# Decay matrices from differences of cumulative decays, with rows spread by DMA

## The chip, the cores and the metric

The kernel runs on one core of a Trainium2 chip. A core has TensorE (PE in the profile; its weight loads are PEld), VectorE (DVE), ScalarE (ACT), GpSimd (POOL) and SyncE (SP, which here only issues DMAs). Each engine works through its own queue in order and waits on semaphores for the others. The metric is the device time of one execution in microseconds; the median of 3 runs of the kernel before is 1635.08 us (1632.72 to 1635.48).

## What is computed

The reference is one layer of a diffusion backbone over 1024 latent tokens and 256 context tokens of width 1024. One input projection feeds two groups of heads: a bidirectional gated DeltaNet (4 heads of 128) and a two-dimensional neighbourhood attention (8 heads of 64); then come an output projection and a SwiGLU block. The change is in the DeltaNet, whose chunked form is, for each head and direction:

```
gam = cumsum(g)                                  # g = log of the decay, within a chunk
decay = exp(where(tril, gam[i] - gam[j], -inf))  # a triangle of decays
m = where(strict, (beta * k) @ k.T * decay, 0)
u, w = solve(I + m, beta * v), solve(I + m, beta * k * exp(gam))
qk = where(tril, q @ k.T * decay, 0)
S, o = scan over the chunks with u, w, qk, gam, and the last gam of a chunk
```

Both directions are scanned; the backward one takes the triangle the other way round. Context chunks come first in each direction. The kernel uses chunks of 128 tokens where the reference has 64, which gives the same sums.

## The kernel before, in words

The kernel is written in a framework that schedules: the Python code says what is computed, and a scheduler sets the order of the instructions on each engine by priorities and estimates of its own. Nearly all DMAs are issued by SyncE, in one queue. A DMA that has to wait (for a free buffer, or for data) holds all DMAs behind it in that queue. Tiles come from pools with a number of buffers for each name; an allocation beyond that number waits until the oldest tile of the name has been used for the last time, its store to memory included.

There are 10 chunks of 128 tokens (2 of context, 8 latent), 4 heads and 2 directions. The tables of one token and head (`G` the log decays, `NB` minus the normalised beta, `EG`, `KD`, `ET` exponentials of sums) are made once by `decay_tables` (L712) for all chunks, with few and small instructions one after the other; `block_inverses` (L765) inverts the 32x32 diagonal blocks of I + m and leaves them in `x_d`. Then `preps` (L854) makes 20 chunk preparations, one for each chunk and direction. A preparation is for all 4 heads at once and consists of:

- `fetch` (L870): loads of the products `kk` (k with k, 4 buffers) and, for a latent chunk, `at` (q with k, 3 buffers), 256 KB each, and of the diagonal blocks `xc` (3 buffers).
- the decay matrix. GpSimd multiplies `G` with a triangular mask into `rg` (L887), once for the high and once for the low part of `G`, 128x512 each. TensorE sums over them with three matmuls of N = 512 into one PSUM bank: two with the mask `mr` (L897), and one with the identity and `mneg` (L898), which adds −1e30 outside the triangle. ScalarE takes the exponential of the bank into the tile `y` (L901, 4 buffers).
- VectorE multiplies `kk` with it for each head (L903) and `at` for all (L906); the decayed `at` is stored to `at_d` (L930).
- the solve: TensorE (L911), a copy by ScalarE (L913), and three rounds of matmuls (L920) and an addition on VectorE (L921) into the same `y`, which is stored to `y_d` (L930). A later part of the kernel reads `y_d` and `at_d`.

At most three preparations are live and one more is fetched. They are generators, advanced between the pieces of the input projection as background work (`bg.step`, 1 to 5 steps at a time). The projection consists of Blocks (matmuls at L389, weights split into a high and a low part, the low part `wlo` by GpSimd at L199) and Wide blocks (L572, `zlo` at L565; their output goes by `nv_d` stores at L583, and copies within memory spread it into `vw_d` at L1024). Context chunks may be prepared early; a latent chunk is fetched only once the blocks of q are done. In the run before, context preparations lie at about 300 to 345 us, latent ones at 425 to 608 us.

Of the kernel before, what the change touches and what calls it, by code (L numbers as in the profile page):

```python
# [26 lines left out]
NCH = T // 128  # L27
NU = NCH * NH
# [5 lines left out]
C_ID, C_LE, C_GE, C_BD2, C_ONE = range(5)  # L34
# [53 lines left out]
def hybrid(ctx, tc, a, dbg):  # L88
# [26 lines left out]
    def const(name, shape, dt=F32):  # L115
        return mid.tile(shape, dt, name=name, tag=name)
# [7 lines left out]
    ident = M[C_ID]  # L124
# [10 lines left out]
    for i, v in enumerate((EPS, -0.5 * math.log(64.0))):  # L135
        dve.memset(bias[:, i:i + 1], v)
    b_eps, b_naq = bias[:, 0:1], bias[:, 1:2]
    mr = const("mr", [128, 5, 128], F32R)
    mneg = const("mneg", [128, 2, 128], F32R)

    v_d = dram.tile([T, 512], F32, name="v_d", tag="v_d")
    k_d = dram.tile([T, 512], F32, name="k_d", tag="k_d")
# [10 lines left out]
    y_d = dram.tile([2, NCH, 128, 4, 128], F32, name="y_d", tag="y_d")  # L153
    at_d = dram.tile([2, 8, 128, 4, 128], F32, name="at_d", tag="at_d")
    x_d = dram.tile([128, 2, 2, NU, 32], F32, name="x_d", tag="x_d")
    x2_d = dram.tile([KT, 128, L], F32, name="x2_d", tag="x2_d")
    f_d = dram.tile([NFB, 2, 128, 512], F32, name="f_d", tag="f_d")
    t_d = dram.tile([NFB, 2, 128, 512], F32, name="t_d", tag="t_d")
# [14 lines left out]
    EG = const("EG", [128, 2, NCH, 4])  # L173
    KD = const("KD", [128, 2, NCH, 4])
    ET = const("ET", [128, 2, NCH, 4])
    act.activation(sc2, c2, AF.Silu)
    bg = Background()

# [181 lines left out]
    with ExitStack() as bs:  # L360
# [242 lines left out]
        with ExitStack() as xs:  # L603
# [26 lines left out]
            wide = xp.tile([128, KT, 32], F32, name="wide", tag="wide")  # L630
            pool.memset(wide, 0.0)
            pool.tensor_copy(wide[:, :, 0:2], sc2)
            pool.tensor_copy(mr[:, 4], ident)
            for d in range(2):
                pool.tensor_scalar(mneg[:, d], masks[:, d], -1.0e30, None, op0=OP.mult)
            pool.tensor_copy(mr[:, 0:4], masks)
            rs = xp.tile([128, T], F32, name="rs", tag="rs")
            acc = xp.tile([128, T], F32, name="acc", tag="acc")
# [73 lines left out]
        def decay_tables(gp):  # L712
            def small(name):
                return gp.tile([128, 2, NCH, 4], F32, name=name, tag=name)
            A, S, E, P2, X = (small(n) for n in ("gA", "gS", "gE", "gP", "gX"))
            nA = gp.tile([128, 8], F32, name="nA", tag="nA")
            act.activation(nA, adt[:, 0:8], AF.Exp)
            dve.tensor_scalar(nA, nA, -1.0, None, op0=OP.mult)
            for d in range(2):
                dtb = adt[:, 8 + 4 * d:12 + 4 * d].rearrange("p (o h) -> p o h", o=1).to_broadcast([128, NCH, 4])  # L720
                dve.tensor_tensor(A[:, d], ab[:, :, 4 * d:4 * d + 4], dtb, OP.add)
            dve.tensor_scalar(X, A, -1.0, None, op0=OP.mult)
            dve.tensor_tensor(X, X, A, OP.max)
# [12 lines left out]
            dve.scalar_tensor_tensor(A, P2, 2.0, A, op0=OP.mult, op1=OP.add)  # L736
            for d in range(2):
                nb = nA[:, 4 * d:4 * d + 4].rearrange("p (o h) -> p o h", o=1).to_broadcast([128, NCH, 4])
                dve.tensor_tensor(G[:, d], A[:, d], nb, OP.mult)
            dve.tensor_scalar(B, B, 1.0, None, op0=OP.add)  # L740
            dve.reciprocal(B, B)

            Y = gp.tile([128, 2, NCH, 4], F32, name="gY", tag="gY")
            dve.tensor_scalar(SV, SV, EPS, None, op0=OP.add)
            rsqrt(Y[:, 0], SV, Y[:, 1])
            dve.tensor_tensor(SV, SV, Y[:, 0], OP.mult)
            dve.tensor_tensor(Y[:, 0], Y[:, 0], Y[:, 0], OP.mult)
            for d in range(2):
                dve.tensor_tensor(B[:, d], B[:, d], Y[:, 0], OP.mult)
            dve.tensor_scalar(NB, B, -1.0, None, op0=OP.mult)  # L750
            dve.tensor_copy(GH, G)
            dve.tensor_tensor(GL, G, GH.bitcast(F32), OP.subtract)
            for _ in range(4):
                yield
            pg = bank()
            for d in range(2):
                g = G[:, d].rearrange("p c h -> p (c h)")
                for q, m in enumerate((M[C_LE + d], mr[:, d].bitcast(F32), M[C_ONE])):
                    o = (q * 2 + d) * NU
# [94 lines left out]
        def preps():  # L854

            first_half.close()
            with ExitStack() as gs:
# [4 lines left out]
                def work(name, bufs=2, dt=F32):  # L862
                    return (pk if name == "kk" else pp).tile([128, 4, 128], dt, name=name, tag=name, bufs=bufs)
# [5 lines left out]
                def fetch(d, c):  # L869

                    kk, xc = work("kk", 4), pp.tile([128, 2, 4, 32], F32, name="xc", tag="xc", bufs=3)
                    sp.dma_start(kk, kk_d[:, c])
                    sp.dma_start(xc, x_d[:, d, :, c * 4:c * 4 + 4])
                    at = None
                    if c >= 2:
                        at = work("at", 3)
                        sp.dma_start(at, qk_d[:, c - 2])
                    return d, c, kk, xc, at

                def prep(n, d, c, kk, xc, at):  # L880
                    lat = c >= 2
                    mle = M[C_LE + d].rearrange("p (o i) -> p o i", o=1).to_broadcast([128, 4, 128])
                    rgs = []
                    for gg in (GH, GL):
                        rg = work("rg", 2, F32R)
                        src = gg.bitcast(F32)[:, d, c].rearrange("p (h o) -> p h o", o=1).to_broadcast([128, 4, 128])
                        pool.tensor_tensor(rg, src, mle, OP.mult)  # L887
                        rgs.append(rg)
                    x0, fx = x0s[n % 3], fxs[n % 2]
                    for b in range(4):  # L890
                        q = slice(b * 32, b * 32 + 32)
                        act.copy(fx[q, :, q], xc[q, 1])
                        pool.tensor_copy(x0[q, :, q], xc[q, 0])
                    yield 1
                    p = bank("pr")
                    for j, rg in enumerate(rgs):
                        pe.matmul(p, mr[:, d], fl(rg), start=j == 0, stop=False)  # L897
                    pe.matmul(p, mr[:, 4], mneg[:, d].rearrange("p (o i) -> p o i", o=1).to_broadcast([128, 4, 128]),  # L898
                              start=False, stop=True)
                    e = work("y", 4)  # L900
                    act.activation(fl(e), p, AF.Exp)  # L901
                    for h in range(4):
                        dve.scalar_tensor_tensor(kk[:, h], kk[:, h], NB[:, d, c, h:h + 1], e[:, h],  # L903
                                                 op0=OP.mult, op1=OP.mult)
                    if lat:
                        dve.tensor_tensor(at, at, e, OP.mult)  # L906
                        stores.append((at_d[d, c - 2], at, tick[0] + 2))
                    yield 1
                    p = bank("pr")
                    for h in range(4):  # L910
                        pe.matmul(p[:, hs[h]], kk[:, h], fx[:, h], start=True, stop=True)  # L911
                    f = kk
                    act.copy(fl(f), p)  # L913
                    yield 1
                    y = e
                    src = x0
                    for _ in range(3):
                        p = bank("pr")
                        for h in range(4):
                            pe.matmul(p[:, hs[h]], f[:, h], src[:, h], start=True, stop=True)  # L920
                        dve.tensor_tensor(fl(y), p, fl(x0), OP.add)  # L921
# [725 lines left out]
```

## Time and profile before

| | us |
|---|---|
| median of 3 runs | 1635.08 (1632.72 to 1635.48) |
| span of the profiled execution | 1634.2 |
| TensorE busy | 1525.4 (93%) |
| VectorE busy | 1037.2 (63%) |
| ScalarE busy | 705.7 (43%) |
| GpSimd busy | 203.0 (12%) |

The profile gives no other time for its execution than the span from the first to the last instruction; the median of the runs is 0.9 us longer. A group's line names the line of the code, the engine, the operation, the tile written and the tiles read, the shape, the number of instructions, then busy time in us and the mean of one in ns, then the idle time of that engine just ahead of them and what ended it. A window's line gives its start and end, its length, and for each engine the busy time and the number of instructions, then the granted TensorE clock as a share of full speed, the share of the DMA engines in use and what they moved in GB/s. In the timeline the columns are the start, the length, the engine, the line, the operation; `[5.59 <-issue]` means 5.59 us of idle time ahead of it, ended by what the arrow names ("issue": by nothing that the profile shows).

### The profile page before, as it was taken

The numbers are of one execution on the slowest core, as the hardware profiler recorded it, in microseconds if no ns is written. First come the engines' busy times: TensorE is split into PE (matmuls) and PEld (weight loads), VectorE is DVE, ScalarE is ACT, GpSimd is POOL, SyncE is SP. The second block draws the span as 40 slices with busy tenths as digits, with TensorE's granted clock in tenths as the row PEclk, the third lists the DMA queues.
The fourth block names the chain that finished last, engine by engine and source line by source line (L and its number), as shares of the span: only waits on it lengthen the run. The fifth ranks groups of instructions, "written<-read, shape, count | busy, mean of one in ns | idle before, by whom it ended". The sixth has DMA issues, their size and how long they took to land.

```text
span 1634.2 us, 24148 instructions
## 1 busy us (share of the span) xinstructions
PE 1525.4 (93%) x8642; PEld 1284.3 (79%) x8642; DVE 1037.2 (63%) x1934; ACT 705.7 (43%) x1340; POOL 203.0 (12%) x275
## 2 busy tenths in 40 slices
PE   3999999999988798999998999999999999999999
PEld 1689787779888786878776787888888888888887
DVE  5855678444364466567898538966565666679752
ACT  5342363663332234565665228433333333445441
POOL 2053611522333220000010000000000000000000
PEclk9998999999999899999998999999999999999999
DMA  9366121535345527999954920532322333798752
GB/s 371 122 195 190 56 75 41 185 120 187 110 131 169 197 93 198 311 276 288 269 175 144 301 102 33 168 123 97 104 97 97 100 107 108 227 364 293 269 162 84
DMA packets 211720, 275.23 MB, mean 168 GB/s; under 512 B 16144, under 2 KB 120080, under 8 KB 210576
## 3 DMA queue, kind: packets, MB, share of 16 engines
q1 hardware_dynamic: 210736, 273.06, 51.6%
q8 instruction: 68, 1.11, 0.3%
q10 hardware_dynamic: 864, 0.63, 0.1%
q14 instruction: 52, 0.43, 0.1%
HBM read 206.78 MB, written 71.04 MB: 170 GB/s over the span
## 4 chain that ended last, share of the span: by engine, by line
PE 64%; DMA 5%; DVE 5%; ACT 3%; issue 2%; SPq 1%; POOL 0%; DVEq 0%; ACTq 0%
PE ps L1219 25%; PE ps L1566 13%; PE blk L389 4%; PE ps L1350 3%; PE blk L572 3%; PE pr L920 2%; PE sc L317 2%; DMA at_d<-at 2%; PE sc L307 2%; PE sc L295 2%; PE ps L1112 1%; DVE cacc L445 1%; PE ps L1372 1%; PE ps L1124 1%; PE pr L911 1%
## 5 line engine op out<-in xcount | busy, mean ns | idle before, releaser
L389 PE MATMUL blk<-hh,whi 128*128 128x512 f32 (+1 forms) x416 | 126.6, 398 | 3.4 <-ACT whi L198 1.6
L389 PE MATMUL blk<-hh,wlo 128*128 128x512 f32 (+1 forms) x416 | 120.4, 383 | 2.3 <-POOL wlo L199 2.3
L1280 ACT CAST uhi<-ws 128x512 fp32r<-128x512 f32 x91 | 54.8, 623 | 151.4 <-PE ps L1219 72.8
L1280 ACT CAST uhi<-wq 128x512 fp32r<-128x512 f32 x101 | 60.6, 621 | 134.9 <-issue 61.6
L389 PE MATMUL blk<-hl,whi 128*128 128x512 f32 (+1 forms) x416 | 117.3, 380 | 0.0
L1281 DVE TENSOR_TENSOR ulo<-wq,uhi 128x512 fp32r<-128x512 f32 x101 | 67.5, 688 | 66.3 <-ACT uhi L1280 36.1
L1219 PE MATMUL ps<-hT,uhi 128*128 128x512 f32 x336 | 104.1, 391 | 3.1 <-ACT hT L1398 3.1
L1219 PE MATMUL ps<-lT,uhi 128*128 128x512 f32 x336 | 104.0, 391 | 0.0
L1219 PE MATMUL ps<-hT,ulo 128*128 128x512 f32 x336 | 103.5, 389 | 0.0
L572 PE MATMUL blk<-zhi,hh 128*128 128x256 f32 (+2 forms) x304 | 90.8, 299 | 0.0
L389 PEld LDWEIGHTS blk<-hh,wlo 128*128 128x128 f32 x416 | 75.2, 196 | 19.2 <-POOL wlo L199 2.8
L1219 PE MATMUL ps<-hB,uhi 128*128 128x512 f32 x288 | 89.7, 392 | 0.0
L1219 PE MATMUL ps<-lB,uhi 128*128 128x512 f32 x288 | 89.3, 391 | 0.0
L1219 PE MATMUL ps<-hB,ulo 128*128 128x512 f32 x288 | 88.8, 389 | 0.0
L572 PE MATMUL blk<-zhi,hl 128*128 128x256 f32 (+2 forms) x304 | 88.4, 291 | 0.0
L572 PE MATMUL blk<-zlo,hh 128*128 128x256 f32 (+2 forms) x304 | 87.9, 289 | 0.0
L389 PEld LDWEIGHTS blk<-hh,whi 128*128 128x128 f32 x416 | 72.7, 198 | 18.4 <-issue 3.6
L389 PEld LDWEIGHTS blk<-hl,whi 128*128 128x128 f32 x416 | 75.0, 196 | 14.1 <-DVE hl L690 0.3
L1281 DVE TENSOR_TENSOR ulo<-ws,uhi 128x512 fp32r<-128x512 f32 x91 | 60.8, 687 | 37.6 <-ACT uhi L1280 29.3
L903 DVE SCALAR_TENSOR_TENSOR kk<-kk,NB,y 128x128 f32<-128x128 f32 x80 | 37.8, 529 | 62.5 <-ACT y L901 62.5
L198 ACT CAST whi<-wraw 128x1024 fp32r<-128x1024 f32 x26 | 27.3, 1049 | 116.0 <-PE blk L389 48.8
L1219 PEld LDWEIGHTS ps<-hT,uhi 128*128 128x128 f32 x336 | 63.0, 188 | 16.3 <-ACT hT L1398 3.5
(333 smaller groups left out, 3778.3 us busy)
## 6 DMA issues: line engine op xcount, KB each, us to landing
wq<-w_fo SPq DMA_DIRECT2D x99, 256.0 KB
wq<-w_gu SPq DMA_DIRECT2D x88, 256.0 KB
wad<-wa SPq DMA_DIRECT2D x64, 256.0 KB
bt<-rpb SPq DMA_DIRECT2D x64, 192.0 KB
t_d<-g SPq DMA_DIRECT2D x22, 512.0 KB
fr<-t_d SPq DMA_DIRECT2D x44, 256.0 KB
f_d<-g SPq DMA_DIRECT2D x33, 256.0 KB
fr<-f_d SPq DMA_DIRECT2D x33, 256.0 KB
```

Of the source, the lines that this page charges most:

```text
L295: pe.matmul(sc[:, u * 640 + n0:u * 640 + n1], q, ks[i], start=i == 0, stop=i == 1)
L307: pe.transpose(sc[:, u * 640 + j * 128:u * 640 + (j + 1) * 128], bt[:, j * 128:(j + 1) * 128], ident)
L317: pe.matmul(sc[u * ND:u * ND + ND, 1280:1408], vv, pt[:, j * 128:(j + 1) * 128], start=j == 0, stop=j == 4)
L389: pe.matmul(o, ww[:, k], xx[k][:, s], start=k == 0 and j == 0, stop=k == KT - 1 and j == end)
L572: pe.matmul(p[:, :c1 - c0], x[k][:, s], ww[:, k, c0:c1], start=k == 0 and j == 0, stop=k == KT - 1 and j == 2)
L903: dve.scalar_tensor_tensor(kk[:, h], kk[:, h], NB[:, d, c, h:h + 1], e[:, h], op0=OP.mult, op1=OP.mult)
L920: pe.matmul(p[:, hs[h]], f[:, h], src[:, h], start=True, stop=True)
L1219: pe.matmul(o, w[wi][:, k], x[xi][:, k], start=first and k == 0 and j == 0, stop=k == n - 1 and j == 2, skip_group_check=True)
L1280: act.copy(hi, self.raw[key])
L1281: dve.tensor_tensor(lo, self.raw[key], hi.bitcast(F32), OP.subtract)
L1350: pe.matmul(o, w[wi][:, k], parts[xi][k][:, s], start=k == 0 and j == 0, stop=k == KT - 1 and j == 2)
L1566: pe.matmul(o[b], w[wi][:, b], F[xn, p][xi], start=n in (0, 1, 5) and p == 0 and j == 0, stop=p == NFB // 2 - 1 and j == 2, skip_group_che ...
```

## The change

The decay matrix is taken from differences of cumulative sums. `decay_tables` clamps `G` from below at −110 and keeps the negated sum `GN` for each token; it also transposes the sums, so that each chunk and head is a row of 128, and stores these 80 rows in memory (`g_d`). `fetch` loads the four rows of a chunk, 2 KB, into all 128 partitions of `e` (a `y` tile, now allocated at the fetch, with 5 buffers), 256 KB in SBUF. GpSimd's affine_select fills −1e30 outside the triangle, in place. ScalarE takes the exponential for each head, 128x128, with the column of `GN` as a bias. The three matmuls, `rg` and `mneg` are gone, and `mr` loses its fifth slice; the rest of the preparation is as it was.

```diff
-    mr = const("mr", [128, 5, 128], F32R)
-    mneg = const("mneg", [128, 2, 128], F32R)
+    mr = const("mr", [128, 4, 128], F32R)
...
+    g_d = dram.tile([2 * NU, 128], F32, name="g_d", tag="g_d")
...
+    GN = const("GN", [128, 2, NCH, 4])
...
-            pool.tensor_copy(mr[:, 4], ident)
-            for d in range(2):
-                pool.tensor_scalar(mneg[:, d], masks[:, d], -1.0e30, None, op0=OP.mult)
...
+            dve.tensor_scalar(G, G, -110.0, None, op0=OP.max)
...
+            gn = GN.rearrange("p d c h -> p (d c h)")
+            act.activation(gn, pg[:, :2 * NU], AF.Copy, scale=-1.0)
+            yield
+            p, rows = bank(), gp.tile([128, 128], F32, name="rows", tag="rows")
+            pe.transpose(p[:2 * NU, :128], gn, ident)
+            act.activation(rows[:2 * NU], p[:2 * NU, :128], AF.Copy, scale=-1.0)
+            sp.dma_start(g_d, rows[:2 * NU])
             yield
...
                     sp.dma_start(xc, x_d[:, d, :, c * 4:c * 4 + 4])
+                    e = work("y", 5)
+                    u = (d * NCH + c) * 4
+                    sp.dma_start(fl(e), g_d[u:u + 4].rearrange("h t -> (h t)").partition_broadcast(128))
                     at = None
...
-                    mle = M[C_LE + d].rearrange("p (o i) -> p o i", o=1).to_broadcast([128, 4, 128])
-                    rgs = []
-                    for gg in (GH, GL):
-                        rg = work("rg", 2, F32R)
-                        src = gg.bitcast(F32)[:, d, c].rearrange("p (h o) -> p h o", o=1).to_broadcast([128, 4, 128])
-                        pool.tensor_tensor(rg, src, mle, OP.mult)
-                        rgs.append(rg)
+
+                    pool.affine_select(e, e, pattern=[[0, 4], [1 - 2 * d, 128]], compare_op=OP.is_ge, fill=-1.0e30,
+                                       base=0, channel_multiplier=2 * d - 1)
...
-                    p = bank("pr")
-                    for j, rg in enumerate(rgs):
-                        pe.matmul(p, mr[:, d], fl(rg), start=j == 0, stop=False)
-                    pe.matmul(p, mr[:, 4], mneg[:, d].rearrange("p (o i) -> p o i", o=1).to_broadcast([128, 4, 128]),
-                              start=False, stop=True)
-                    e = work("y", 4)
-                    act.activation(fl(e), p, AF.Exp)
+                    for h in range(4):
+                        act.activation(e[:, h], e[:, h], AF.Exp, bias=GN[:, d, c, h:h + 1])
```

The change also moves instructions. On TensorE the preparations' first matmuls leave the blocks. In a Block of the projection before, with `blk` its banks, `hh` the high part of the activations and `pr` the preparation's bank, there stood:

```order
L389 MATMUL blk_3486<-hh0_133,wlo_3147 128x512
L897 MATMUL pr_3521<-rg_3502,mr_83 128x512
L897 MATMUL pr_3521<-rg_3504,mr_83 128x512
L898 MATMUL pr_3521<-mneg_84,mr_83 128x512
L389 MATMUL blk_3484<-hh1_135,whi_3146 128x256
```

In the changed kernel no such matmul stands there; the preparation's next ones (L911) come in the same Block:

```order
L390 MATMUL blk_3485<-hh1_136,wlo_3148 128x256
L390 MATMUL blk_3486<-hh1_136,wlo_3148 128x512
L390 MATMUL blk_3487<-hh1_136,wlo_3148 128x512
L911 MATMUL pr_3563<-fx0_2314,kk_3497 128x128 x4
L390 MATMUL blk_3485<-hh2_138,whi_3147 128x256
L390 MATMUL blk_3486<-hh2_138,whi_3147 128x512
```

The L911 matmuls of the first latent chunk now stand where the three matmuls of its decay matrix stood.

On VectorE, after the normalisation of q (`RQ2`), the first latent chunks stood like this before (`y` is the decay matrix, at L921 the solve's tile):

```order
L903 SCALAR_TENSOR_TENSOR kk_3496<-kk_3496,NB_115,y_3525 128x128 x4
L906 TENSOR_TENSOR at_3500<-at_3500,y_3525 128x512
L903 SCALAR_TENSOR_TENSOR kk_3514<-kk_3514,NB_115,y_3570 128x128 x4
L906 TENSOR_TENSOR at_3518<-at_3518,y_3570 128x512
L921 TENSOR_TENSOR y_3525<-pr_3605,x01_2298 128x512
L903 SCALAR_TENSOR_TENSOR kk_3553<-kk_3553,NB_115,y_3621 128x128 x4
L906 TENSOR_TENSOR at_3557<-at_3557,y_3621 128x512
L921 TENSOR_TENSOR y_3525<-pr_3637,x01_2298 128x512
```

In the changed kernel the same place reads:

```order
L1033 TENSOR_TENSOR RQ2_110<-RQ_109 128x32
L906 TENSOR_TENSOR at_3503<-at_3503,y_3501 128x512
L906 TENSOR_TENSOR at_3522<-at_3522,y_3520 128x512
L906 TENSOR_TENSOR at_3560<-at_3560,y_3558 128x512
L906 TENSOR_TENSOR at_3604<-at_3604,y_3602 128x512
L906 TENSOR_TENSOR at_3747<-at_3747,y_3745 128x512
L921 TENSOR_TENSOR y_3501<-pr_3607,x01_2312 128x512
```

The products L903 of the first four of them have moved some 40 rows up, ahead of the last convolutions (L442, L446) and just behind the context chunks.

On SyncE, in the second half of the latent chunks, the queue read before:

```order
L877 DMA at_4398<-qk_d_91 128x512
L583 DMA nv_d_92<-zt_4244 128x256
L872 DMA kk_4335<-kk_d_90 128x512
L930 DMA y_d_97<-y_4051 128x512
L873 DMA xc_4459<-x_d_99 128x2x128
L872 DMA kk_4394<-kk_d_90 128x512
L930 DMA y_d_97<-y_4116 128x512
```

In the changed kernel, in the copies' part, with the row loads (L882) between:

```order
L1024 DMA vw_d_94<-nv_d_91 128x1x512 x4
L930 DMA at_d_97<-at_4455 128x512
L878 DMA kk_4608<-kk_d_89 128x512
L930 DMA y_d_96<-y_4133 128x512
L879 DMA xc_4691<-x_d_98 128x2x128
L886 DMA at_4696<-qk_d_90 128x512
L930 DMA at_d_97<-at_4614 128x512
L882 DMA y_4650<-g_d_99 128x512
L878 DMA kk_4646<-kk_d_89 128x512
L930 DMA y_d_96<-y_4332 128x512
```

The loads of rows stand behind stores of `y` that they need a buffer from (the row load into y_4650 takes the buffer of y_4133, whose store stands five rows ahead), the `vw_d` copies come four in a row, and the loads and stores of `at` stand two to three chunks further ahead of those copies.

More of the change, by code (lines that the diff above doesn't have):

```diff
@@ L877, in fetch, with prep @@
                         sp.dma_start(at, qk_d[:, c - 2])
-                    return d, c, kk, xc, at
-                def prep(n, d, c, kk, xc, at):
+                    return d, c, kk, xc, e, at
+                def prep(n, d, c, kk, xc, e, at):
                     lat = c >= 2
-                    mle = M[C_LE + d].rearrange("p (o i) -> p o i", o=1).to_broadcast([128, 4, 128])
-                    rgs = []
-                    for gg in (GH, GL):
-                        rg = work("rg", 2, F32R)
-                        src = gg.bitcast(F32)[:, d, c].rearrange("p (h o) -> p h o", o=1).to_broadcast([128, 4, 128])
-                        pool.tensor_tensor(rg, src, mle, OP.mult)
-                        rgs.append(rg)
+                    pool.affine_select(e, e, pattern=[[0, 4], [1 - 2 * d, 128]], compare_op=OP.is_ge, fill=-1.0e30,
+                                       base=0, channel_multiplier=2 * d - 1)
                     x0, fx = x0s[n % 3], fxs[n % 2]
```

## The prediction

> **What bounds the kernel now.** I read the page's first section, then a table of windows over the chunk preparations, then the waits, the chain and single pieces of the timeline there.
>
> ```profile
> span 1634.2 us, 24148 instructions
> PE 1525.4 (93%) x8642; PEld 1284.3 (79%) x8642; DVE 1037.2 (63%) x1934; ACT 705.7 (43%) x1340; POOL 203.0 (12%) x275
> ```
>
> TensorE is busy for 93% of the span, so work taken off TensorE is worth something only where TensorE is what the others wait for. Preparations run in two places, so I cut those into windows.
>
> ```profile
> core 0: us, PE busy (x) PEld busy (x) DVE busy (x) ACT busy (x) POOL busy (x), PEclk, DMA share, GB/s
> 300.00:345.00 45.00, 40.48 (x221) 32.91 (x220) 20.18 (x32) 27.02 (x50) 26.00 (x45) 0.96 0.50 151
> 425.00:450.00 25.00, 22.08 (x123) 18.86 (x122) 11.20 (x15) 10.06 (x19) 13.34 (x9) 0.86 0.43 136
> 450.00:475.00 25.00, 21.49 (x140) 19.78 (x141) 15.46 (x22) 7.07 (x17) 10.53 (x18) 0.93 0.50 154
> 475.00:517.00 42.00, 40.66 (x330) 39.07 (x329) 27.44 (x47) 16.75 (x38) 12.74 (x24) 1.00 0.46 148
> 517.00:575.00 58.00, 44.12 (x281) 39.91 (x281) 19.38 (x39) 12.85 (x33) 16.02 (x30) 0.87 0.54 181
> 575.00:608.00 33.00, 32.17 (x198) 27.45 (x197) 20.62 (x31) 9.06 (x12) 5.84 (x7) 0.97 0.20 70
> ```
>
> Two stretches (475 to 517, 575 to 608) are TensorE's, idle for 1.3 and 0.8 us. From 425 to 475 it idles 50 − 22.08 − 21.49 = 6.4 us, from 517 to 575 58 − 44.12 = 13.9 us. The chain that ended last and SyncE's waits say what those 13.9 us wait for:
>
> ```profile
> 517.08 9.42 DMA at_d<-at
> 540.23 10.88 DMA at_d<-at
> 554.12 10.39 DMA at_d<-at
> 565.43 4.32 DMA y_d<-y
> ```
> ```profile
> SPq L877 <- DMA at_d<-at: 43.3, 10, 8.1
> ```
>
> A store of a decayed product (`at_d`) takes 9 to 11 us here, because it shares the DMA engines with the copies into `vw_d`; the next load into that `at` buffer waits for it on SyncE, and behind it stand the `kk` loads and `y_d` stores. TensorE sees it as two gaps:
>
> ```profile
> 531.50 1.20 PE L911 MATMUL pr<-fx,kk 128*128 128x128 f32 x4 [5.59 <-issue]
> ...
> 570.86 2.08 PE L911 MATMUL pr<-fx,kk 128*128 128x128 f32 x8 [7.38 <-DVE kk L903]
> ```
>
> **The matmuls that go.** Each of 20 preparations loses two matmuls of L897 and one of L898. What they hold of TensorE is the distance from their start to the next matmul's:
>
> ```profile
> 481.96 0.63 PE L897 MATMUL pr<-rg,mr 128*128 128x512 f32 x2
> 482.42 0.39 PE L898 MATMUL pr<-mneg,mr 128*128 128x512 f32 x1
> 482.65 0.28 PE L572 MATMUL blk<-zhi,hh 128*128 128x256 f32 x1
> ```
>
> 482.65 − 481.96 = 0.69 us. The windows of L897 alone (two matmuls a preparation) say where they lie:
>
> ```profile
> 475.00:517.00 42.00, 2.77 (x8) 1.22 (x8) 1.00 0.46 148
> 517.00:575.00 58.00, 4.22 (x10) 1.95 (x10) 0.87 0.54 181
> 575.00:608.00 33.00, 1.78 (x4) 0.96 (x4) 0.97 0.20 70
> ```
>
> Five are in the stretch that is bound by stores; there they fill time that is idle anyway, and I cost them at nothing. The other 15 are worth 15 × 0.69 = 10.4 us. If only the six in the two stretches that are full counted, 4.1 us; if all the busy time of the two lines did, 16.6 + 8.9 = 25.5 us (groups, 300 to 610 us):
>
> ```profile
> L887 POOL TENSOR_TENSOR rg<-GL,cst 128x512 fp32r<-128x512 f32 x20 | 21.2, 1062 | 0.2 <-PE pr L897 0.2
> L887 POOL TENSOR_TENSOR rg<-GH,cst 128x512 fp32r<-128x512 f32 x20 | 21.1, 1055 | 49.5 <-PE pr L897 49.1
> L897 PE MATMUL pr<-rg,mr 128*128 128x512 f32 x40 | 16.6, 486 | 2.1 <-POOL rg L887 2.0
> L898 PE MATMUL pr<-mneg,mr 128*128 128x512 f32 x20 | 8.9, 447 | 0.0
> L901 ACT ACTIVATE y<-pr 128x512 f32<-128x512 f32 x20 | 11.9, 596 | 29.7 <-PE pr L898 20.8 <-DMA y_d<-y 8.7
> ```
>
> I take −10.4, since the busy sum counts the overlap of neighbours twice (0.63 + 0.39 us in the rows above, for 0.69).
>
> **The first latent preparations come earlier.** They no longer need TensorE for the exponent, and on VectorE the first four products with `kk` stand ahead of the last convolutions, 40 rows earlier. What TensorE waits for from 425 to 475 us is such work:
>
> ```profile
> 438.71 1.16 PE L920 MATMUL pr<-x,kk 128*128 128x128 f32 x8 [1.39 <-ACT kk L913]
> ...
> 451.44 1.16 PE L911 MATMUL pr<-fx,kk 128*128 128x128 f32 x8 [1.54 <-DVE y L921]
> ```
>
> Bounds 0 and −6.4; the solve's own sequence (L911, L913, three rounds) stays, and both rows are of it, so −4. What is late next there is L921 on VectorE.
>
> **The stretch bound by stores.** Its ends are −13.9 (all idle time goes) and +30.7 (the three landings of 9.42, 10.88 and 10.39 us come once more). For a gain: the loads and stores of `at` stand two or three chunks further ahead of the `vw_d` copies, so about the two gaps of 5.59 and 7.38 us shrink, less 2 for what the order leaves: −11. Against it: five row loads of 256 KB now fall there, 1.31 MB at the 181 GB/s of the window, 7.2 us. Net −4; nearer to no change than to either end, since the same queue carries the same stores and more.
>
> **The row loads and SyncE.** An issue takes 0.32 us (rows below), so 20 loads take 6.4 us on a queue that does not hold TensorE outside the stretch above. From the sixth latent chunk on, the load needs a `y` buffer that a `y_d` store has to leave, and the store stands two to five places ahead on the same queue. Queued behind the wait are a load of `kk`, stores of `at` and `y` and the Wide blocks' `nv_d` stores. Undisturbed, a store is done in 2.0 us, and `kk` is early by 15 us:
>
> ```profile
> 481.14 0.32 SPq L930 DMA_DIRECT2D at_d<-at  x1
> 483.15 0.32 SPq L877 DMA_DIRECT2D at<-qk_d  x1
> ```
> ```profile
> 454.92 0.32 SPq L872 DMA_DIRECT2D kk<-kk_d  x1
> ```
> ```profile
> 469.93 1.13 DVE L903 SCALAR_TENSOR_TENSOR kk<-kk,NB,y 128x128 f32<-128x128 f32 x4
> ```
>
> So I cost the wait at nothing; the cover is the preparation two or three chunks ahead, and without it each of 11 loads shows up.
>
> **Exponentials.** One of 596 ns becomes four of 128x128 with a pointer as bias; the nearest rows have such an operand:
>
> ```profile
> L1116 ACT ACTIVATE vk<-ps,KN 128x128 f32<-128x128 f32 x64 | 18.7, 371 | 7.5 <-PE ps L1112 7.3
> ```
>
> 20 × (4 × 0.371 − 0.596) = 17.8 us more on ScalarE, which is busy for 40% from 475 to 517 us. ScalarE also evicts TensorE's banks, so a delay of 0.9 us can meet one: +1 (0 to +17.8).
>
> **GpSimd's triangle.** Two products of 1.06 us become one affine_select of 128x512, which the trace does not have. Nearest below is a memset, nearest above a cast of that size:
>
> ```profile
> L867 POOL MEMSET x<- 128x512 f32 x3 | 1.5, 542 | 0.0
> ...
> L636 POOL CAST mr<-masks 128x512 fp32r<-128x512 f32 x1 | 1.7, 1675 | 0.0
> ```
>
> I take 1.1 us, as the product of that size has: GpSimd gains 1 us a chunk and stays off the path, 0. But the select waits for a DMA now, and behind it in program order stand the low parts of weights (`wlo`) that TensorE needs; they have been ahead by whole blocks, so 0.
>
> The Trainium skill (GPSIMD Engine Reference, section 3.1 Elementwise) puts data-dependent branching at about 12 cycles for each element; if the triangle were done so, 512 × 12 / 1.2 GHz is an estimate of 5.1 us for one. No run here shows it, and by it the sum would be that of rival (d).
>
> **VectorE.** Its products run at 347 ns or, beside GpSimd, up to 2460:
>
> ```profile
> L903 DVE SCALAR_TENSOR_TENSOR kk<-kk,NB,y x80: 339/347/2460, 307.8 to 598.6; 128x128 f32<-128x128 f32 x80
> ```
>
> They add up to 37.8 us, 37.8 − 80 × 0.347 = 10 us above the median. With GpSimd's two-input products gone some of that goes: −1 (−10 to 0), as VectorE is mostly off the path.
>
> The Trainium skill (GPSIMD Engine Reference, section 1 Specifications) says that GpSimd shares its SBUF interface with VectorE where that reads two SBUF inputs. The spread of 339 to 2460 ns agrees; by that rule the one-input select would disturb them too, and the sum would be 1 us higher.
>
> **Decay tables.** A clamp, two copies, a transpose and a store of rows come into a serial chain before the preparations, beside TensorE's projection blocks: +0.5 (0 to +3, five steps of some 0.6 us, the exp's 596 ns). The matmul mask's cast and two products at the start leave GpSimd when nobody waits for it: 0.
>
> **Sum.** −10.4 − 4 − 4 + 1 − 1 + 0.5 = −17.9; 1634.2 − 17.9 = 1616.3. The median of the runs, 1635.08 us, is 0.9 above the span, so 1617.
>
> **Rivals.** (a) Both idle stretches vanish, because they were only late preparations: −10.4 − 6.4 − 13.9 + 0.5 = −30.2, 1605. For it: L903 and `issue` end both long gaps. Against: the stores of `at` behind `vw_d` remain.
>
> (b) Gains cancel: ScalarE's delay (up to +17.8) eats them, 1635. Against: ScalarE's share.
>
> (c) SyncE blocks. The row load's wait for the `y_d` store costs 2.0 us in the open and 4.3 (chain, 565 us) to 10.9 in the `vw_d` copies. SyncE already waits through much of this part, so a delay passes to all behind it. It decides when the delays piled up exceed the 15 us that `kk` is early. Eleven loads, six at 2.0 and five at 7.6 (the mean of 4.32 and 10.88) are 50 us; less 15 of cover and the 18 to 23 gained elsewhere, +12: 1647.
>
> (d) The triangle is slow. If one takes three times the cast, 5 us, 20 take 100 us on GpSimd against the 42 of the two products now. Most hides, but in 517 to 575 us, where kk, y and the triangle wait on each other, five show with what they have over the present pair, 5 × (5 − 2.1) = 14.5, and half of the 17.9 is lost because the early start goes: +5.5, 1640. It decides from about 3 us for one. Against: both rows of that size are under 1.7 us.
>
> **How the numbers follow.** Chances: the forecast 0.42 (own range 1608 to 1630), (a) 0.11, (b) 0.08, (c) 0.25, (d) 0.14. A measurement here tells 0.2% (3 us) from no change: the three runs spread by 0.17%. Faster takes the forecast and (a), 0.53; same is (b), 0.08; slower is (c) and (d), 0.39. The range reaches from just below (a), 1604, to just past (c), 1648, and leaves out the upper ends of the unknown costs when several meet.
>
> **What would show it.** Right: no L897 and L898, 475 to 517 shorter by four times 0.69, the gaps at 438 and 451 mostly gone, affine_select near 1.1 us, four exps of about 0.37 us. Wrong: SyncE waiting at L882 for `y_d<-y` for more than 30 us, with TensorE idle at L911 behind it (c); affine_select above 3 us (d); ScalarE's exps releasing TensorE's banks (b); or the waits for `at_d<-at` as long as before, so that the −4 is nothing.

## The result and the profile after

The changed kernel takes 1637.2 us (median of 20 runs, 1629.75 to 1641.82) against 1633.45 us before (20 runs, 1628.27 to 1635.48): a ratio of 1.0031, 95% interval 1.0021 to 1.0040. It is slower by 0.3%, where 1617 us and a gain were forecast.

The two profiled executions, one of each kernel, do not show that difference (spans of 1633.1 us after and 1634.2 before), but they show where the expected gain went. The page of the changed kernel, first section:

```profile
span 1633.1 us, 24115 instructions
PE 1510.2 (92%) x8583; PEld 1274.3 (78%) x8583; DVE 1024.2 (63%) x1935; ACT 718.0 (44%) x1402; POOL 174.0 (11%) x252
```

TensorE works 15 us less, and the span is 1.1 us shorter. The windows over the preparations, in the columns that the prediction's table has for the kernel before:

```profile
300.00:345.00 45.00, 41.54 (x227) 34.06 (x226) 22.73 (x40) 36.33 (x74) 22.11 (x43) 0.96 0.70 212
425.00:450.00 25.00, 22.64 (x163) 20.71 (x162) 6.81 (x10) 8.61 (x21) 7.43 (x4) 1.00 0.63 206
450.00:475.00 25.00, 20.40 (x142) 18.87 (x141) 16.61 (x27) 10.87 (x29) 7.78 (x16) 0.93 0.57 180
475.00:517.00 42.00, 35.52 (x275) 34.77 (x275) 17.75 (x35) 15.89 (x41) 6.92 (x19) 0.92 0.59 191
517.00:575.00 58.00, 39.14 (x246) 35.96 (x245) 18.29 (x42) 13.61 (x43) 8.96 (x25) 0.82 0.54 173
575.00:608.00 33.00, 32.07 (x211) 27.99 (x210) 17.53 (x22) 8.98 (x16) 4.92 (x9) 1.00 0.22 75
```

From 425 to 608 us TensorE is now idle for 33.2 us (the sum of length minus busy), before for 22.5. The time that the matmuls gave back became idle time: the stretch from 475 to 517 us, which had 1.3 us of it, has 6.5, and from 425 to 475 us it is 7.0 where it was 6.4. What TensorE waits for there (waits of TensorE, 425 to 612 us: total, times, longest):

```profile
PE pr L920 <- DVE y L921: 15.1, 9, 5.0
PE pr L920 <- ACT kk L913: 11.3, 3, 7.3
PE pr L920 <- issue: 6.1, 3, 2.7
```

The same view of the kernel before (425 to 610 us) has for the first of them:

```profile
PE pr L920 <- DVE y L921: 0.8, 2, 0.6
```

The rounds of the solve wait for VectorE's addition of the round before. VectorE was not busy: its own waits in the changed kernel name loads.

```profile
DVE kk L903 <- DMA kk<-kk_d: 23.3, 4, 8.5
DVE at L906 <- DMA at<-qk_d: 19.2, 4, 11.2
```

Neither stood in the waits of before (425 to 610 us), where VectorE waited for the exponential instead:

```profile
DVE kk L903 <- ACT y L901: 57.9, 13, 16.0
```

With that long wait TensorE still waited only 0.8 us for additions, and the order is another: from 425 us on VectorE ran two chunks' products, one addition, a third chunk's products and seven additions. In the changed kernel five products L906 run first, and later single products stand between the additions. One place in the timeline, from SyncE, VectorE and TensorE in turn, tells how it goes:

```profile
513.75 0.54 SPq L878 DMA_DIRECT2D kk<-kk_d  x1
```
```profile
522.97 0.35 DVE L903 SCALAR_TENSOR_TENSOR kk<-kk,NB,y 128x128 f32<-128x128 f32 x1 [7.28 <-DMA kk<-kk_d]
523.24 0.68 DVE L921 TENSOR_TENSOR y<-pr,x 128x512 f32<-128x512 f32 x1
...
525.06 0.67 DVE L921 TENSOR_TENSOR y<-pr,x 128x512 f32<-128x512 f32 x1
```
```profile
525.78 2.08 PE L920 MATMUL pr<-y,kk 128*128 128x128 f32 x8 [5.04 <-DVE y L921]
```

A load of `kk`, issued at 513.75 us, lands 9.2 us later, behind four `vw_d` copies issued from 507.2 us on. VectorE's queue holds products L903 of a later chunk, which wait for that load, ahead of two additions L921 of earlier chunks, whose matmuls were done by 520 us. The additions run at 523.24 and 525.06, TensorE's next round waits for the second at the head of its queue, and the Wide block's matmuls behind wait too. The gap costs more than its length. The granted clock is 1.00 from 515 to 520 us, 0.78 from 520 to 525 and 0.54 from 525 to 530, and eight matmuls of L920 that took 1.06 us at 518.74 take 2.08 behind the gap.

SyncE shows what the prediction's rival on row loads expected, and the `at` wait that it started from has shrunk (waits of SyncE, 425 to 610 us):

```profile
SPq L882 <- DMA y_d<-y: 20.2, 8, 6.8
...
SPq L886 <- DMA at_d<-at: 10.6, 4, 7.2
```

The new instructions themselves are cheap (groups, 300 to 620 us):

```profile
L901 ACT ACTIVATE y<-y,GN 128x128 f32<-128x128 f32 x80 | 26.2, 391 | 51.2 <-POOL y L892 51.0
...
L892 POOL TENSOR_SCALAR_AFFINE_SELECT y<-y 128x512 f32<-128x512 f32 x20 | 13.5, 675 | 43.2 <-DMA y<-g_d 37.8 <-ACT cacc L423 2.3 <-PE pr L920 1.5
```

### The profile page after: what moved, and what is told of

Its sections match the earlier page's. It is cut to its first block, busy times and chain, and to the rows that moved or that the text cites. A ratio compares the mean times of both kernels' runs of the same rounds, so it can differ in the third digit from the quotient of the medians.

```text
span 1633.1 us, 24115 instructions
## 1 busy us (share of the span) xinstructions
PE 1510.2 (92%) x8583; PEld 1274.3 (78%) x8583; DVE 1024.2 (63%) x1935; ACT 718.0 (44%) x1402; POOL 174.0 (11%) x252
## 4 chain that ended last, share of the span: by engine, by line
PE 71%; DVE 9%; DMA 8%; ACT 6%; issue 2%; POOL 2%; SPq 1%; DVEq 0%; POOLq 0%; ACTq 0%
PE ps L1219 26%; PE ps L1566 13%; PE blk L390 10%; PE ps L1350 3%; PE blk L573 3%; PE sc L318 2%; PE sc L308 2%; DVE tt L831 2%; DMA y<-g_d 2%; PE sc L296 1%; DVE N L833 1%; PE pr L920 1%; DMA kk<-kk_d 1%; PE ps L1112 1%; DMA wad<-wa 1%
## 5 line engine op out<-in xcount | busy, mean ns | idle before, releaser
L390 PE MATMUL blk<-hh,whi 128*128 128x512 f32 (+1 forms) x416 | 128.1, 402 | 3.5 <-ACT whi L199 1.6
L390 PE MATMUL blk<-hh,wlo 128*128 128x512 f32 (+1 forms) x416 | 117.6, 377 | 2.3 <-POOL wlo L200 2.3
L390 PE MATMUL blk<-hl,whi 128*128 128x512 f32 (+1 forms) x416 | 118.0, 382 | 0.0
L390 PEld LDWEIGHTS blk<-hh,wlo 128*128 128x128 f32 x416 | 75.1, 196 | 18.7 <-POOL wlo L200 2.9
L390 PEld LDWEIGHTS blk<-hl,whi 128*128 128x128 f32 x416 | 76.0, 198 | 15.1 <-issue 0.7
L390 PEld LDWEIGHTS blk<-hh,whi 128*128 128x128 f32 x416 | 72.0, 199 | 17.8 <-issue 3.2
L1219 PEld LDWEIGHTS ps<-lT,uhi 128*128 128x128 f32 x336 | 63.4, 189 | 13.3
L1219 PEld LDWEIGHTS ps<-hT,ulo 128*128 128x128 f32 x336 | 63.4, 189 | 13.3
```

The source lines that it names most:

```text
L390: pe.matmul(o, ww[:, k], xx[k][:, s], start=k == 0 and j == 0, stop=k == KT - 1 and j == end)
L1219: pe.matmul(o, w[wi][:, k], x[xi][:, k], start=first and k == 0 and j == 0, stop=k == n - 1 and j == 2, skip_group_check=True)
```

## The experiments

The theories as they stand in the expectations: A, row loads wait for stores of y, and that is all; B, the rows' traffic; C, TensorE's slots were never worth anything; and, formed from the traces of the first four runs, D: products and exponentials moved ahead in the queues of VectorE and ScalarE wait there for loads, and the solves behind them wait with them. Ratios are to the kernel before, with their 95% intervals, and differences in us are worked out from them unless medians are named. To compare: the changed kernel has 1.0031.

**8 buffers for y**

```diff
-                    e = work("y", 5)
+                    e = work("y", 8)
```

> The changed kernel with 8 buffers for y in place of 5, so that the row load of a chunk needs the buffer of a chunk three further back. Theory A (the freed TensorE time is lost because row loads wait for stores of y: SyncE waited 22.7 us in 9 waits at L882, GpSimd 37.8 us for the rows): the waits at L882 go below 5 us, TensorE's idle time from 425 to 608 us falls from 33 to about 20 us, the time falls by 8 to 14 us against the changed kernel, to about 0.995 of the kernel before. Theory B (the rows' traffic beside the vw_d copies costs, whatever the buffers): within 3 us of the changed kernel, 1.003. Theory C (the stretch is bound by at_d stores and the solve's chain, TensorE's slots were never worth anything): 1.003 too, with the at_d or kk loads as the last wait.

Measured: 1645.16 us, 1.0085 (1.0070 to 1.0100), worse than with 5. SyncE's waits at L882 from 425 to 610 us fell from 20.2 to 11.3 us, as theory A has it, but TensorE (first row) and VectorE (second) waited longer:

```profile
PE pr L920 <- DVE y L921: 20.4, 10, 9.4
```
```profile
DVE kk L903 <- DMA kk<-kk_d: 38.0, 9, 10.5
```

With more buffers the rows came earlier (the thirteenth load at 460.3 us in place of 482.1), the scheduler put the products further ahead (eight products L906 stand ahead of the fourth addition, five in the changed kernel), and VectorE's waits for `kk` grew from 23.3 to 38.0 us. A was wrong as the whole cause.

**Without the row loads**

```diff
-                    sp.dma_start(fl(e), g_d[u:u + 4]...partition_broadcast(128))
...
-                    pool.affine_select(e, e, ...)
+                    src = GP[:, d, c].rearrange("p (h o) -> p h o", o=1).to_broadcast([128, 4, 128])
+                    pool.affine_select(e, src, ...)
```

> The changed kernel without its row loads: GpSimd's select reads a resident tile in place of the loaded rows (the decay matrix is then 1 in the triangle, which is left out of the computation: the spread of the rows), one more small copy in the tables. The y tile still needs its buffer, now at GpSimd. Theory A (SyncE's queue is held by the row loads): a gain of 8 to 14 us against the changed kernel, 0.994 to 0.998 of before. Theory B (traffic): the same gain, so this run tells A and B from C only, and the run with 8 buffers tells A from B. Theory C: within 3 us of the changed kernel, 1.003.

Measured: 1627.75 us, 0.9970 (0.9959 to 0.9981), 10 us below the changed kernel (0.0061 of 1633). The loads cost that much together with what they hold up. TensorE's rounds (L921 in this kernel) still wait for VectorE's additions (L922), longer than in the changed kernel (425 to 612 us), so the row loads are not what makes that wait. The run also shows that products placed early need not cost more than the change gains, since with that wait it is still 0.3% faster than the kernel before:

```profile
PE pr L921 <- DVE y L922: 27.3, 8, 12.6
```

**The kernel before without its matmuls**

```diff
-                    pe.matmul(p, mr[:, d], fl(rg), ...)      # and the one with mneg
-                    act.activation(fl(e), p, AF.Exp)
+                    act.activation(fl(e), fl(rgs[0]).bitcast(F32), AF.Exp)
```

> The kernel before without the three matmuls of the decay matrix: ScalarE takes the exponential of GpSimd's product directly (the sum over the triangle is left out of the computation). No row loads, 4 buffers of y, one exponential. It measures the matmuls' slots and the earlier start by themselves. The prediction's steps: -10.4 for slots and -4 for the early start, 0.990 to 0.994. Theory C (slots worth nothing): 0.999 to 1.001.

Measured: 1642.94 us, 1.0070 (1.0055 to 1.0084). Taking 60 matmuls away, with no row load, made the kernel 11 us slower; neither the prediction nor C had that. ScalarE, VectorE and TensorE at one place of it:

```profile
525.26 0.63 ACT L896 ACTIVATE y<-rg 128x512 f32<-128x512 f32 x1 [16.88 <-DMA y_d<-y]
```
```profile
525.92 3.56 DVE L898 SCALAR_TENSOR_TENSOR kk<-kk,NB,y 128x128 f32<-128x128 f32 x4 [12.99 <-ACT y L896]
```
```profile
531.78 2.08 PE L915 MATMUL pr<-y,kk 128*128 128x128 f32 x8 [14.55 <-DVE y L916]
```

The exponential waits for a buffer of y, that is for a store; the product behind it in time stands on VectorE ahead of an earlier chunk's addition L916; TensorE waits 14.55 us for that addition. Once the exponential does not need TensorE, the scheduler puts the products ahead, whether rows are loaded or not. What they wait for here is mostly a store that has to leave a buffer (51.2 us on ScalarE from 425 to 612 us), in the changed kernel mostly a load. This led to theory D.

**The kernel before with the new tables**

```diff
+            dve.tensor_scalar(G, G, -110.0, None, op0=OP.max)
...
+            act.activation(gn, pg[:, :2 * NU], AF.Copy, scale=-1.0)
+            yield
+            pe.transpose(p[:2 * NU, :128], gn, ident)      # and the copy and store of the rows
```

> The kernel before with the additions to the decay tables alone (clamp, negated copy, one more step, transpose, copy, store of the rows). The traces show the first preparations 4.3 us later after the change (first kk load at 302.6 against 298.4 us). If the tables did that and it stays: +3 to +4 us, 1.002 to 1.003. The prediction's term was +0.5 us, 1.000. If the delay has another cause or is made good later: 1.000.

Measured: 1635.01 us, 1.0019 (1.0008 to 1.0030): +3.1 us. The first preparation starts at 302.6 us, as in the changed kernel, against 298.4 in the kernel before (loads of `kk`: first and last start; here, then before):

```profile
L882 SPq DMA_DIRECT2D kk<-kk_d x20: 319/379/966, 302.6 to 571.9; - x20
```
```profile
L872 SPq DMA_DIRECT2D kk<-kk_d x20: 319/376/1164, 298.4 to 567.5; - x20
```

**One small step put back**

```diff
+                    p = bank("pr")
+                    pe.matmul(p[:, :4], ident, GN[:, d, c], start=True, stop=True)
+                    gb = pp.tile([128, 4], F32, name="gb", tag="gb", bufs=4)
+                    act.copy(gb, p[:, :4])
                     for h in range(4):
-                        act.activation(e[:, h], e[:, h], AF.Exp, bias=GN[:, d, c, h:h + 1])
+                        act.activation(e[:, h], e[:, h], AF.Exp, bias=gb[:, h:h + 1])
```

> The changed kernel with one small step put back: a matmul of 4 columns passes the bias column through TensorE and PSUM, and ScalarE copies it out before the exponentials. With it the scheduler puts the products L903 and L906 back behind the solves of the chunks before, as in the kernel before; row loads, select, four exponentials and 5 buffers stay. Theory D (products moved ahead on VectorE wait there for loads of kk and at, 42 us in the changed kernel, and the solves' additions behind them make TensorE wait 15 us): VectorE's waits for kk and at loads vanish, TensorE's waits for L921 fall to about 1 us as before, and the time is 8 to 12 us below the changed kernel, 0.996 to 0.998 of before. Theory A (row loads wait for y stores): the waits at L882 stay at some 20 us, no gain, 1.002 to 1.004.

Measured: 1628.23 us, 0.9966 (0.9950 to 0.9982). Twenty more matmuls and copies made the changed kernel 0.65% faster. TensorE's wait for the additions (L925 here; 300 to 660 us) is gone, VectorE's for `kk` loads is small (425 to 612 us), and SyncE still waits at the row loads, about half as long (425 to 610 us):

```profile
PE pr L924 <- DVE y L925: 0.9, 3, 0.6
```
```profile
DVE kk L907 <- DMA kk<-kk_d: 5.2, 1, 5.2
```
```profile
SPq L882 <- DMA y_d<-y: 11.3, 6, 3.1
```

That is D's result and not A's, and VectorE's order is nearly that of the kernel before again: products of two chunks, one addition, the third chunk's products (with one addition among them), seven additions. Of TensorE's waits one of 13.2 us at L915, the first matmuls of a solve, is left. The step acts on ScalarE too, since the exponentials stand behind the small matmul, and the loads move with them; the run does not part these.

**The same with 7 buffers for y**

```diff
-                    e = work("y", 5)
+                    e = work("y", 7)
```

> The same with 7 buffers of y. Theory D: with the order held, more buffers do no harm as they did alone (1.0085); 0.994 to 0.998. Theory A: the buffers bring the gain, at least 5 us below the run with 5. If more buffers harm by traffic or by the queue, whatever VectorE's order, it is at 1.003 or above.

Measured: 1617.24 us, 0.9908 (0.9895 to 0.9920), 9.5 us below the run with 5. So theory A is right too, but only with the order held: the stretch from 517 to 575 us (with 5 buffers, then with 7) gets TensorE back.

```profile
517.00:575.00 58.00, 39.31 (x237) 36.06 (x238) 19.29 (x42) 17.91 (x58) 8.14 (x21) 0.79 0.53 177
```
```profile
517.00:575.00 58.00, 45.09 (x291) 40.66 (x290) 26.31 (x51) 18.50 (x56) 9.78 (x20) 0.88 0.54 182
```

Alone, more buffers cost 9 us (8 of them); with the order held, 7 bring as much. The longest wait of TensorE that is left, 10.9 us, is for a product L907 whose load of `kk` is late (VectorE waits 13.4 us for it). In every run the difference is made before the projection ends: its last matmul (L389 or L390) starts at 635.8 us before, 634.5 in the changed kernel, 628.1 with the step and 619.2 here, and what follows takes 996 to 1002 us in each.

**The products on GpSimd**

```diff
-                    for h in range(4):
-                        dve.scalar_tensor_tensor(kk[:, h], kk[:, h], NB[:, d, c, h:h + 1], e[:, h], ...)
+                    pool.tensor_tensor(kk, kk, nb, OP.mult)
+                    pool.tensor_tensor(kk, kk, e, OP.mult)
...
-                        dve.tensor_tensor(at, at, e, OP.mult)
+                        pool.tensor_tensor(at, at, e, OP.mult)
```

> The changed kernel with the products on GpSimd (three of 128x512 a chunk in place of five instructions on VectorE), so that VectorE never waits for a load ahead of a solve. Theory D: TensorE's waits for L921 fall below 3 us; GpSimd takes the waits and some 60 us more work, and the time is below the changed kernel by 4 to 12 us, unless GpSimd's low parts of weights come late. Theory A: no gain, since the row loads are as late as before, 1.003.

Measured: 1654.71 us, 1.0136 (1.0120 to 1.0153): a miss. TensorE's wait for L921 did fall to 0.9 us, but GpSimd's queue took the place of VectorE's (waits of TensorE, 300 to 660 us; of GpSimd, 425 to 610 us):

```profile
PE pr L920 <- POOL kk L903: 16.5, 3, 8.1
PE pr L920 <- ACT kk L913: 16.1, 5, 8.9
```
```profile
POOL at L906 <- DMA at<-qk_d: 35.3, 2, 32.9
POOL kk L903 <- DMA kk<-kk_d: 28.6, 4, 12.1
```

GpSimd now waits for the loads ahead of products that TensorE waits for, so the waits moved with the products into the other queue. How much of the loss they are is not shown: the products themselves take 69.8 us on GpSimd (300 to 620 us; 38.6 on VectorE in the changed kernel), and a solve waits for them too.

**The kernel before without its matmuls, with the small step**

```diff
                     p = bank("pr")
+                    pe.matmul(p[:, :4], ident, EG[:, d, c], start=True, stop=True)
+                    act.copy(gb, p[:, :4])
-                    act.activation(fl(e), p, AF.Exp)
+                    act.activation(fl(e), fl(rgs[0]).bitcast(F32), AF.Exp, bias=gb[:, 0:1])
```

> The kernel before without its three matmuls (the sum over the triangle left out of the computation), but with the matmul of 4 columns and a small copy in their place. VectorE's order is then that of the kernel before. Theory D: the loss of the run without matmuls (1.007) turns into a gain, 0.993 to 0.997, since the slots are worth 0.5 to 0.7 us each for 10 to 15 chunks. If the slots are worth nothing because other waits end the stretch: 0.999 to 1.001. If it stays at 1.007, VectorE's order isn't the cause.

Measured: 1629.88 us, 0.9977 (0.9965 to 0.9990). The loss of 0.7% without the step is a gain of 0.2% with it. The window from 425 to 608 us of the kernel before, of the run without matmuls and of this one:

```profile
425.00:608.00 183.00, 160.53 (x1065) 145.07 (x1065) 94.10 (x151) 55.79 (x119) 58.47 (x87) 0.93 0.44 143
```
```profile
425.00:608.00 183.00, 140.77 (x997) 131.06 (x997) 90.23 (x134) 51.33 (x113) 53.40 (x82) 0.90 0.44 144
```
```profile
425.00:608.00 183.00, 156.91 (x1064) 141.45 (x1064) 106.87 (x154) 62.40 (x139) 67.76 (x90) 0.94 0.45 147
```

TensorE was idle for 22.5, 42.2 and 26.1 us. Besides the small step itself, the two runs without matmuls differ only in the order that it imposes, on VectorE, where it is nearly that of the kernel before, and on ScalarE, whose exponentials no longer wait long for a buffer of y (5.7 us, from 51.2).

**7 buffers for kk, the order not held**

```diff
-                    kk, xc = work("kk", 4), ...
+                    kk, xc = work("kk", 7), ...
```

> The changed kernel with 7 buffers for kk in place of 4 and nothing else: the products stay ahead on VectorE, but the loads of kk that they wait for can be issued earlier. Theory D (the wait for a load ahead of the solves is what costs): VectorE's waits for kk loads (23 us) mostly vanish, TensorE's waits for L921 halve, 0.997 to 1.001. If only the order matters and another wait (at loads, exponentials) takes the place at once, as with 8 buffers of y: 1.003 to 1.008.

Measured: 1638.51 us, 1.0026 (1.0013 to 1.0039): no gain over the changed kernel. VectorE's waits for `kk` loads are gone, and TensorE's for L921 fell to 4.0 us, but its waits for ScalarE's copy L913 rose from 11.3 to 23.9 (waits of TensorE, then of ScalarE, 425 to 612 us; one place on ScalarE and TensorE):

```profile
PE pr L920 <- ACT kk L913: 23.9, 6, 6.9
PE pr L920 <- DVE y L921: 4.0, 5, 2.1
```
```profile
ACT y L901 <- POOL y L892: 51.3, 9, 15.9
```
```profile
550.26 1.28 ACT L901 ACTIVATE y<-y,GN 128x128 f32<-128x128 f32 x4 [9.64 <-POOL y L892]
551.45 0.56 ACT L913 COPY kk<-pr 128x512 f32<-128x512 f32 x1
```
```profile
552.06 2.07 PE L920 MATMUL pr<-y,kk 128*128 128x128 f32 x8 [4.53 <-ACT kk L913]
```

The same fault shows on ScalarE: exponentials of a later chunk wait for GpSimd's select (which waits for its rows), and the solve's copy waits behind them. With one wait taken away, the next in line takes over.

**The step put back, 7 buffers for y, no extra yield**

```diff
             act.activation(gn, pg[:, :2 * NU], AF.Copy, scale=-1.0)
-            yield
             p, rows = bank(), gp.tile([128, 128], F32, name="rows", tag="rows")
```

> The run with the step put back and 7 buffers of y, without the extra yield in the decay tables (the transpose of the rows follows at once). If the 3 us that the tables cost by themselves come from the extra step of the background work, 2 to 3 us below that run, 0.989. If they come from the instructions: no change, 0.991.

Measured: 1614.39 us, 0.9881 (0.9862 to 0.9900), the fastest of all. It is 2.9 us below the run with the yield by the medians, as expected, though the intervals overlap a little (0.9895 to 0.9920 there); against the next run, which has the yield and 4 buffers of `at`, it is 3.0 us.

**The same with the yield, and 4 buffers for at**

```diff
-                        at = work("at", 3)
+                        at = work("at", 4)
```

> The run with the step put back and 7 buffers of y, with 4 buffers of at in place of 3. SyncE still waits 23.9 us in 8 waits at the loads of at for stores of at. If these hold the stretch with the copies into vw_d, 4 to 8 us below that run, 0.986 to 0.988; if other waits end last there, 0.991.

Measured: 1617.41 us, 0.9899 (0.9885 to 0.9914): no change from 3 buffers (0.9908). SyncE's waits there fell from 23.9 to 18.7 us, and nothing came of it.

**The control: 4 buffers for at in the kernel before**

```diff
-                        at = work("at", 3)
+                        at = work("at", 4)
```

> The control: the kernel before with 4 buffers of at in place of 3 and nothing else. SyncE waited 43.3 us in 10 waits at those loads, which the prediction took as the bound of the stretch from 517 to 575 us. If they are, 6 to 14 us faster than before, 0.991 to 0.996; if the next wait (y_d stores ahead of the exponential, 8.7 us) takes over, 0.998 to 1.000.

Measured: 1632.32 us, 0.9997 (0.9983 to 1.0012): no change. SyncE's waits for `at_d` (43.3 us before) are 37.1:

```profile
SPq L877 <- DMA at_d<-at: 37.1, 9, 8.2
```

One more buffer leaves most of that wait standing, so the run does not take it away; it shows that a buffer more buys nothing.

## Why the prediction was wrong

The step that failed is "The first latent preparations come earlier", which had −4 us since "They no longer need TensorE for the exponent". The order was read rightly and its sign wrongly. The place of an instruction in an in-order queue was taken as a gain where its input is early; the prediction did not ask what stands behind a product that is placed early and whose load is late. From 425 to 475 us, where −6.4 was the bound of the gain, TensorE idles 7.0 us. For VectorE the prediction named as late next only L921 itself; the runs show L921 behind a product that waits for a load. The cost of the moved order is what the small step takes away: 1.0031 to 0.9966, 10.6 us with the row loads in, and 1.0070 to 0.9977, 15 us, without them. It is no fixed price: the run without row loads has early products too, and its ratio is 0.9970. Gaps were also counted by their length alone, where the matmuls behind one ran at about half speed (2.08 us for 1.06).

That 1637 us lies between the times of rivals (b), 1635, and (d), 1640, is luck. The triangle of (d) is fast, and (b)'s gains were to be lost to the time that the exponentials take, not to what they wait for.

- The matmuls' slots: −10.4 forecast. With the order held they are worth −3.8 us (0.9977; 1.6 to 5.7 by the interval), with a small matmul and a copy in their place. With the order lost, nothing of them was left (1.0070). That a slot on a TensorE busy for 97% is time, as the term took it, holds only where the solve keeps up.
- The stretch from 517 to 575 us: −4 forecast, from loads of `at` that wait for stores of `at`. That wait fell from 43.3 to 10.6 us and the stretch became idler (13.9 to 18.9 us). So that release alone did not bound the stretch in the changed kernel. Whether it did before stays open: 4 buffers of `at` took only 6.2 of the 43.3 us away there, and changed the time neither there nor in the kernel with the step and 7 buffers of y.
- Row loads and SyncE: costed at nothing, with cover of 15 us. The wait came (22.7 us in 9 waits between 300 and 620 us, against 50 in rival (c)), and the cover did not hide it: with the order held, two more buffers bring 9.5 us. Rival (c) had the mechanism, on SyncE, but not the size, 1647 us; and by itself its cure, more buffers, made the kernel slower.
- Exponentials: 0.391 us each against 0.371, as forecast. Their +1 us was a count of time; what the traces show is their place ahead of the copy L913 in ScalarE's queue. At 547.77 us four of them, which waited 9.90 us for the select, hold up a copy for which TensorE waits 7.34 us. Such waits are 1.4 us before, 11.3 in the changed kernel and 23.9 with 7 buffers of `kk`.
- The triangle: 0.675 us for one, below the 1.1 taken and far from the 5 us of rival (d). The Trainium skill (GPSIMD Engine Reference, section 3.1 Elementwise) puts data-dependent branching at about 12 cycles for an element; the trace shows no such price for this select.
- VectorE: −1 forecast. Its products fell from 37.8 to 27.6 us, by the whole upper bound of 10 us, and the kernel got no faster, as VectorE is busy for only 77 of the 183 us from 425 to 608. The rule of the Trainium skill on the shared interface (GPSIMD Engine Reference, section 1 Specifications) was read as 1 us more for the select; their sum did not grow.
- Decay tables: +0.5 forecast, +3.1 measured. The extra yield is probably most of it: the run without it is 2.9 us faster by the medians, with intervals that overlap. It stands in the change and was not costed as a step.

The prices of the new instructions, one by one, were near; the terms on what stands behind an instruction were not. What stays open: how the 10.6 us divide between VectorE's and ScalarE's queue (each has its waits in the trace, but no run holds one alone); how much of the run without row loads is traffic; and what the step would bring there, since why early products cost 15 us in the kernel before without its matmuls, and less in that run, was not tested.

## What to carry to other kernels

An instruction that loses its dependence on the busiest engine can be moved ahead by a scheduler, and if it waits there for a load or a buffer, everything behind it in that in-order queue waits too: after such a change, look at what stands behind each early instruction, not at how early it is. A dependence can be worth keeping for the order that it imposes; a matmul of 4 columns and a small copy in place of three matmuls of 512 kept it here and turned 1.0031 into 0.9966. Without that, 8 buffers of y made things worse and 7 of `kk` brought nothing; with it, 7 buffers of y brought 9.5 us, so try buffers after the order.

## What was not expected of the hardware

A 256 KB load issued behind copies within memory landed 9.2 us after its issue (513.75 to 522.97 us), where an undisturbed store of that size had taken 2.0. The select of 128x512 on GpSimd took 633 to 1160 ns, mean 675, less than the 1.06 us of a product of that size. VectorE's products got faster when GpSimd's two-input products were gone: 387 ns in the mean against 529. The other runs agree whatever the order: 386 to 413 without those products (no row loads, the step put back, 7 buffers of `kk`), 610 and 707 with them (the two runs of the kernel before without matmuls).
